# A hybrid decoder's two layers on one core: raw tiles transposed in pairs between the layers, and a memory norm shared by both

## The chip, the cores and the metric

The kernel runs on one core of one Trainium2 chip. A time is the time on the device of one execution, in microseconds (us); a profile is one more execution, recorded instruction by instruction. In the profile PE is the matrix engine (TensorE), PEld its loading of weights, DVE the vector engine (VectorE), ACT the scalar engine (ScalarE), POOL is GpSimd, and SP is SyncE, which mostly issues transfers (DMAs). Each engine works through its own instructions in order and waits on semaphores for the others.

## The reference, cut to what matters

The activations x are 512 rows of 1024 numbers in float32, the memory is 256 rows of 1024.

```python
def rmsnorm(x, g):
    y = x * rsqrt(mean(x * x, axis=-1) + EPS)
    return y * g

for layer in range(2):
    h = rmsnorm(x, g_mix_pre[layer])
    f = fox_shortconv_mixer(h, ...) if layer == 0 else rglru_mixer(h, c_w_in, ...)
    x = x + rmsnorm(f, g_mix_post[layer])
    m = rmsnorm(mem, g_mem[layer])
    f = memory_cross_attention(rmsnorm(x, g_cross_pre[layer]), m, w_xq, w_xkv, w_xo)
    x = x + rmsnorm(f, g_cross_post[layer])
    f = swiglu(rmsnorm(x, g_ffn_pre[layer]), w_ffn_gu, w_ffn_down)
    x = x + rmsnorm(f, g_ffn_post[layer])
```

Layer 0 mixes with forgetting attention and a short convolution, layer 1 with a recurrent block whose first step is the product of h with `c_w_in` (1024 x 2048). The memory `mem` is the same in both layers; only the weights `g_mem[layer]` differ.

## The kernel before

**Numbers.** Every product of matrices is made in three: each operand is split into a high part (a copy in the matrix format, made by ACT: `hTh`, `wh`, `rh`, `mTh`) and a low part (operand minus high part, made by DVE: `hTl`, `wl`, `rl`, `mTl`), and PE runs high x high, high x low and low x high into one bank of PSUM (`mm3`).

**Tiles.** x stays in SBUF as four tiles of 128 rows, `x[0]` to `x[3]`. A norm takes the sum of squares of each half of a row (`junk` on ACT), two small DVE operations and a power on POOL (`rstd`; its name is `pre` or `post`), and then a scaling on DVE, `scaled` (L256), which multiplies by the row's factor and by the norm's weights in one operation per 512 columns. The scaled rows `h` are transposed by PE (`put_T`, L303, two banks of 4 transposes for a tile), and ACT and DVE split each bank of 128x512 at once (L312, L313). `half 0` below is tiles 0 and 1, `half 1` is tiles 2 and 3; a group of 24 matmuls of 128x256 makes one bank of a half.

**The output stage.** `DownProj.run` is the last product of a layer. It runs the rows in pairs of tiles, over a sequence of groups for which a table `at[g]` says what ACT and DVE do beside PE's matmuls of group g. The last groups (`late`) are run tile by tile at its end: tile 2's remainder, then tile 3's. c is the sum of a part of the result, `gain` multiplies it by the weights of the norm behind it (`yb` is such a product), `root` is `rstd`, `add` adds it to x (L813). In layer 0 (`more`) the stage goes on into the first product of layer 1: it squares, scales and transposes each new tile of x, and loads and splits the first weights of `c_w_in` in four pieces n = 0 to 3 (`hi_f` is load and cast on ACT, L777, `lo_f` the difference on DVE, L781). `hook(m)` is called by that product after its group m of half 0 and transposes tiles 2 and 3; group m = 3 is the last, then half 1 begins. In layer 1 (`final`) `add` also writes the output.

**The memory.** In each layer `memory_rows` loads and normalizes the memory, and `memory_T` transposes it (two steps of 8 transposes of 128x128, L971) and splits it; the steps run within the mixer's output product.

**Order.** In these stages each engine runs its instructions in the order in which the code issues them; the tables and the order of calls set it. Buffers come from rings: an instruction that writes to a buffer waits until the last reader of its earlier content is done. Loads of weights are issued by SP, each as soon as its buffer is free.

Of the kernel before, what the change touches and what calls it, by code (L numbers as in the profile page):

```python
# [15 lines left out]
P = 128  # L16
# [4 lines left out]
MEM = 256  # L21
# [21 lines left out]
def trunk_kernel(ctx: ExitStack, tc: tile.TileContext, a: dict, out: bass.AP):  # L43
# [103 lines left out]
    def spend(n, behind=None):  # L147
# [14 lines left out]
        ("scw", a["ab_conv_w"][0].rearrange("j (m p) -> (j m) p", p=P)),  # L162
    )
# [135 lines left out]
    def put_T(hT, t, hs, bank=bankB):  # L299
        for hf in range(2):  # L300
            ps = bank()
            for j in range(4):
                nc.tensor.transpose(  # L303
                    out=ps[:, j * P:(j + 1) * P], in_=hs[hf][:, j * P:(j + 1) * P], identity=ident
                )
            v = ps.rearrange("p (k c) -> p k c", k=4)
            sl = slice(t * P, (t + 1) * P)
            if hT.raw:
                nc.scalar.copy(out=hT.raw[hf][:, :, sl], in_=v)
            hi, lo = dst_T(hT, hf, t)  # L310
            last = (
                nc.scalar.copy(out=hi, in_=v).ins,  # L312
                nc.vector.tensor_tensor(out=lo, in0=v, in1=f(hi), op=ALU.subtract).ins,  # L313
            )
        return last

# [324 lines left out]
    class DownProj(OutProj):  # L641
# [183 lines left out]

        def run(self):
# [39 lines left out]
            for t in range(2):  # L866
# [5 lines left out]
                if not self.final:  # L872
                    do(g + 2, lambda t=t: self.square_x(t))
                    do(g + 4, lambda t=t: self.root(t))
                    do(g + 5, lambda t=t: self.scale(t))
# [22 lines left out]
            if more:  # L898
                self.hi_f(0)
                self.transpose(0)  # L900
                self.hi_f(1)
# [3 lines left out]
            if more:  # L905
                self.transpose(1)
            self.gain(1, q[0], yb[0])
            self.root(2)
            if more:
                self.lo_f(0)  # L910
            self.add(2, (p1[0], yb[0]))
            if more:
                self.square_x(2)
                self.hi_f(2)
                self.lo_f(1)
                self.root(2)
                self.hi_f(3)
            for s in late[2:]:
                self.mms(s, (1,), bk[6])
            total(1)  # L920
            self.gain(1, q[1], yb[1])
            if more:
                self.scale(2)
            self.root(3)
            if more:
                self.lo_f(2)
            self.add(3, (p1[1], yb[1]))
            if more:
                self.square_x(3)
                self.lo_f(3)  # L930
                self.root(3)

        def hook(self, m):
            if m == 1:
                self.transpose(2)
                self.scale(3)
            elif m == 2:
                self.transpose(3)


    def memory_rows(layer, gate):

        with tc.issue_after(gate) if gate else nullcontext():
            g = load_gain(a["g_mem"][layer])
        mg = group("mem")
        for t in range(2):
# [8 lines left out]
            for hf in range(2):  # L955
                nc.vector.scalar_tensor_tensor(
                    out=mt[hf], in0=mt[hf], scalar=r, in1=g[hf], op0=ALU.mult, op1=ALU.mult
                )
        return mg

    def memory_T(mg, bank):

        ghi, glo = group("mTh"), group("mTl")
        vhi = ghi.rearrange("p a (b c) -> p (a b) c", c=MEM)
        vlo = glo.rearrange("p a (b c) -> p (a b) c", c=MEM)

        def step(t):
            for hf in range(2):
# [5 lines left out]
                v = ps.rearrange("p (k c) -> p k c", k=4)  # L974
                dst = (slice(None), slice(hf * 4, hf * 4 + 4), slice(t * P, (t + 1) * P))
                nc.scalar.copy(out=vhi[dst], in_=v)
                nc.vector.tensor_tensor(out=vlo[dst], in0=v, in1=f(vhi[dst]), op=ALU.subtract)

        return vhi, vlo, (lambda: step(0), lambda: step(1))
# [556 lines left out]
    for layer in range(2):  # L1536
# [11 lines left out]
        vhi, vlo, steps = memory_T(memory_rows(layer, pm.gate), pm.first)  # L1548
# [40 lines left out]
```

## Time and profile before

| | |
|---|---|
| median of 3 runs | 1395.26 us (1394.58 to 1395.35) |
| the profiled execution's own time | 1394.71 us |
| its span in the profile | 1392.9 us |
| mean granted clock of PE | 0.997 of full speed |
| PE busy | 1378.2 us, 99% of the span |
| DVE busy | 1116.3 us, 80% |
| ACT busy | 720.2 us, 52% |
| POOL busy | 111.1 us, 8% |

In a row of the timeline stand the start in us, the duration, the engine, the line of the kernel, the operation, output and inputs by name, and their size; xN is N instructions in a row, and a bracket holds the idle time of the engine just before and what ended it. In a group's row stand busy time and mean duration in ns behind the bar. The boundary between the layers lies at 710 to 750 us, the memory steps of layer 0 at 210 to 235 us, those of layer 1 at 850 to 885 us, and the last output stage ends the span. The first product of layer 1, half 0, begins at 728.5 us.

### The profile page before, as it was taken

Reading aid. Unit: us, or ns where it says so; the run is one execution under the profiler, and the core shown is the slowest. Engines: PE = TensorE matmul, PEld = TensorE weight load, DVE = VectorE, ACT = ScalarE, POOL = GpSimd, SP = SyncE. Lnnn points to the kernel's source line nnn. Section 1 sums busy time; section 2 is a strip of 40 time slices with the busy share of each in tenths; the row PEclk is TensorE's granted clock in tenths of the full one; section 3 lists DMA queues with packets and bytes.
Section 4 is the critical chain, followed back from the end, with each engine's and each line's share of the span. In section 5 each row is a group of like instructions: output and inputs, shape, how many; then the busy total and the mean of one; then the engine's idle time right before and its main releaser. Section 6 shows DMA issues by size and latency. Waiting matters only on the chain.

```text
span 1392.9 us, 21792 instructions
## 1 busy us (share of the span) xinstructions
PE 1378.2 (99%) x8432; PEld 1227.8 (88%) x8432; DVE 1116.3 (80%) x1801; ACT 720.2 (52%) x1175; POOL 111.1 (8%) x162
## 2 busy tenths in 40 slices
PE   8999999999999999999999999999999999999998
PEld 6778788888899999998879888888889999999886
DVE  6876678546589999989898998754558999999987
ACT  4354455534464444456664796543446444445663
POOL 1000001012010101000010000101200010000001
PEclk9999999999999999999999999999999999999999
DMA  6845452669224557567656657267822555656664
GB/s 224 277 155 159 137 181 57 202 164 177 66 92 142 163 143 196 160 241 222 195 159 210 222 181 242 73 199 163 164 67 91 166 150 151 177 168 233 205 188 144
DMA packets 156066, 233.61 MB, mean 168 GB/s; under 512 B 8549, under 2 KB 90545, under 8 KB 154938
## 3 DMA queue, kind: packets, MB, share of 16 engines
q1 hardware_dynamic: 135138, 180.25, 40.3%
q0 software_dynamic: 16928, 45.11, 15.0%
q10 hardware_dynamic: 3896, 6.86, 1.5%
q8 instruction: 66, 1.08, 0.3%
q14 instruction: 38, 0.31, 0.1%
HBM read 220.64 MB, written 57.69 MB: 200 GB/s over the span
## 4 chain that ended last, share of the span: by engine, by line
PE 95%; DVE 3%; issue 1%; DMA 1%; ACT 0%; POOL 0%; SPq 0%; DVEq 0%; POOLq 0%; ACTq 0%
PE bA L319 14%; PE bA L321 14%; PE bA L320 14%; PE bB L319 6%; PE bB L320 6%; PE bB L321 6%; PE bB L795 2%; PE bB L794 2%; PE bB L793 2%; PE bA L552 2%; PE bA L554 2%; PE bB L554 2%; PE bA L553 2%; PE bB L553 2%; PE bB L552 2%; PE bA L795 2%
## 5 line engine op out<-in xcount | busy, mean ns | idle before, releaser
L529 DVE TENSOR_TENSOR wl<-st,wh 128x1024 fp32r<-128x1024 f32 x108 | 131.4, 1222 | 99.1 <-ACT wh L528 98.1
L528 ACT CAST wh<-st 128x1024 fp32r<-128x1024 f32 x108 | 113.4, 1051 | 122.4 <-PE bA L320 70.6
L319 PE MATMUL bA<-hTh,wh 128*128 128x512 f32 (+1 forms) x448 | 171.9, 384 | 0.0
L321 PE MATMUL bA<-hTh,wl 128*128 128x512 f32 (+1 forms) x448 | 168.9, 377 | 2.3 <-DVE wl L781 2.3
L320 PE MATMUL bA<-hTl,wh 128*128 128x512 f32 (+1 forms) x448 | 168.2, 375 | 0.0
L420 ACT CAST wg<-wr 128x1024 fp32r<-128x1024 f32 x80 | 83.7, 1046 | 49.2 <-DVE wr L449 38.5
L759 ACT CAST wh<-st 128x1024 fp32r<-128x1024 f32 x76 | 74.9, 985 | 63.6 <-PE bA L795 27.0
L321 PEld LDWEIGHTS bA<-hTh,wl 128*128 128x128 f32 x448 | 84.8, 189 | 18.4 <-DVE wl L781 2.8
L421 DVE TENSOR_TENSOR wg<-wr,wg 128x1024 fp32r<-128x1024 f32 x80 | 97.4, 1217 | 0.0
L320 PEld LDWEIGHTS bA<-hTl,wh 128*128 128x128 f32 x448 | 85.0, 190 | 13.6
L319 PEld LDWEIGHTS bA<-hTh,wh 128*128 128x128 f32 x448 | 85.0, 190 | 13.4
L764 DVE TENSOR_TENSOR wl<-st,wh 128x1024 fp32r<-128x1024 f32 x76 | 86.7, 1140 | 10.1 <-ACT wh L759 10.1
L420 ACT CAST wh<-tt 128x1024 fp32r<-128x1024 f32 x40 | 42.1, 1053 | 61.5 <-DVE tt L449 61.5
L319 PE MATMUL bA<-hTq,wh 128*128 128x256 f32 x208 | 59.2, 284 | 0.0
L321 PE MATMUL bA<-hTq,wl 128*128 128x256 f32 x208 | 58.8, 283 | 0.0
L320 PE MATMUL bA<-hTq,wh 128*128 128x256 f32 x208 | 58.8, 283 | 0.0
L793 PE MATMUL bB<-wh,ya 128*128 128x512 f32 x148 | 57.6, 389 | 0.0
L794 PE MATMUL bB<-wl,ya 128*128 128x512 f32 x148 | 57.6, 389 | 0.0
L795 PE MATMUL bB<-wh,ya 128*128 128x512 f32 x148 | 57.6, 389 | 0.0
L739 DVE TENSOR_TENSOR ya<-yb,ya 128x512 fp32r<-128x512 f32 x84 | 53.9, 645 | 0.0
L793 PE MATMUL bA<-wh,ya 128*128 128x512 f32 x132 | 51.3, 389 | 0.0
L794 PE MATMUL bA<-wl,ya 128*128 128x512 f32 x132 | 51.3, 389 | 0.0
(372 smaller groups left out, 4434.8 us busy)
## 6 DMA issues: line engine op xcount, KB each, us to landing
wr<-in_w_ffn_gu_dram SPq DMA_DIRECT2D x80, 512.0 KB, 5.5
st<-t SPq DMA_DIRECT2D x40, 512.0 KB, 4.2
t<-in_w_ffn_down_dram SPq DMA_DIRECT2D x32, 512.0 KB, 5.1
st<-in_w_xkv_dram SPq DMA_DIRECT2D x32, 512.0 KB, 4.7
st<-in_w_ffn_down_dram SPq DMA_DIRECT2D x30, 512.0 KB, 3.4
st<-in_ab_w_in_dram SPq DMA_DIRECT2D x24, 512.0 KB, 4.7
y<-yr POOLq DMA_DIRECT2D x18, 512.0 KB, 4.2
t<-in_w_ffn_down_dram POOLq DMA_DIRECT2D x16, 512.0 KB, 8.4
```

Source lines behind the costliest of these rows:

```text
L319: nc.tensor.matmul(out=ps, lhsT=wh, rhs=xh, start=first, stop=False)
L320: nc.tensor.matmul(out=ps, lhsT=wh, rhs=xl, start=False, stop=False)
L321: nc.tensor.matmul(out=ps, lhsT=wl, rhs=xh, start=False, stop=last)
L420: return (lambda: nc.scalar.copy(out=to[0], in_=src), lambda: nc.vector.tensor_tensor(out=to[1], in0=src, in1=f(to[0]), op=ALU.subtract))
L421: lambda: nc.vector.tensor_tensor(out=to[1], in0=src, in1=f(to[0]), op=ALU.subtract))
L528: nc.scalar.copy(out=hi, in_=src)
L529: nc.vector.tensor_tensor(out=lo, in0=src, in1=f(hi), op=ALU.subtract)
L759: nc.scalar.copy(out=self.wt[s][0], in_=self.st[s])
L764: nc.vector.tensor_tensor(out=lo, in0=self.st[s], in1=f(hi), op=ALU.subtract)
L793: nc.tensor.matmul(out=banks[t], lhsT=yh, rhs=wh[:, jj, :], start=first and jj == 0, stop=False)
L794: nc.tensor.matmul(out=banks[t], lhsT=yh, rhs=wl[:, jj, :], start=False, stop=False)
L795: nc.tensor.matmul(out=banks[t], lhsT=yl, rhs=wh[:, jj, :], start=False, stop=last and jj == n - 1)
```

## The change

- **Pairs of raw tiles (layer 0's output stage).** Tiles 0 and 1 are scaled by ACT with the row's factor alone (`scale_raw`). `put_T_pair` transposes two blocks of 128 columns of both tiles into one bank, four times (j = 0 to 3), and ACT and DVE split each block k in a 128x256 operation of its own, which also multiplies by the weight of the norm ("gp", one number per partition).
- **The next weights.** `hi_f` 0 and 1 move ahead of the squares of the last sums; `lo_f` 0 and 1 come ahead of the first pairs, pieces 2 and 3 later.
- **The order of the tail.** The last matmuls (`late[2:]`) are issued ahead of the gain of tile 2, `total(1)` ahead of `add(2)`, in both layers; in layer 0 `scale(2)` comes behind `add(3)`, and the hook runs one group later.
- **The memory.** Layer 0 scales the rows by the row's factor alone, keeps the transposed rows as `mTr`, writes them to DRAM (`memT`, 1 MB) and splits `mTr` with the weights of `g_mem[0]` ("gm") in 8 parts. Layer 1 loads `memT` and splits it with those of `g_mem[1]`; its norm and its transposes are gone, as are the loads of g_mem spread over all partitions.

```diff
@@ vectors loaded at the start, one number per partition
+        ("gm", a["g_mem"].rearrange("l (m p) -> (l m) p", p=P)),
+        ("gp", a["g_mix_pre"][1].rearrange("(m p) -> m p", p=P)),
...
+    def put_T_pair(hT, hss, j, gain):
+        ps = bankB()
+        for kk in range(2):
+            for t in range(2):
+                c = 2 * kk + t
+                src = hss[t][j // 2][:, (j % 2 * 2 + kk) * P:(j % 2 * 2 + kk + 1) * P]
+                nc.tensor.transpose(out=ps[:, c * P:(c + 1) * P], in_=src, identity=ident)
+        for kk in range(2):
+            k, v = 2 * j + kk, ps[:, kk * 256:kk * 256 + 256]
+            hi, lo, g = hT.hi[k][:, 0:256], hT.lo[k][:, 0:256], ch(gain, k)
+            nc.scalar.mul(out=hi, in_=v, mul=g)
+            nc.vector.scalar_tensor_tensor(out=lo, in0=v, scalar=g, in1=f(hi), op0=ALU.mult, op1=ALU.subtract)
...
+        def scale_raw(self, t):
+            self.hs[t] = [sbuf("h") for _ in range(2)]
+            for hf, h in enumerate(self.hs[t]):
+                nc.scalar.mul(out=h, in_=x[t][:, hf * 512:(hf + 1) * 512], mul=self.r[t])
...
-                    do(g + 5, lambda t=t: self.scale(t))
+                    do(g + 5, lambda t=t: self.scale_raw(t))
+            if not self.final:
+                do(6 * N + 1, lambda: [self.hi_f(n) for n in range(2)])
...
             if more:
-                self.hi_f(0)
-                self.transpose(0)
-                self.hi_f(1)
+                for n in range(2):
+                    self.lo_f(n)
+                self.pairs(0, 1)
             for s in late[:2]:
                 self.mms(s, (1,), bk[6])
             total(0)
             if more:
-                self.transpose(1)
+                for n in range(2):
+                    self.hi_f(2 + n)
+                self.lo_f(2)
+                self.pairs(2, 3)
+            for s in late[2:]:
+                self.mms(s, (1,), bk[6])
             self.gain(1, q[0], yb[0])
             self.root(2)
+            total(1)
             if more:
-                self.lo_f(0)
+                self.lo_f(3)
             self.add(2, (p1[0], yb[0]))
             if more:
                 self.square_x(2)
-                self.hi_f(2)
-                self.lo_f(1)
-                self.root(2)
-                self.hi_f(3)
-            for s in late[2:]:
-                self.mms(s, (1,), bk[6])
-            total(1)
             self.gain(1, q[1], yb[1])
-            if more:
-                self.scale(2)
             self.root(3)
             if more:
-                self.lo_f(2)
+                self.root(2)
             self.add(3, (p1[1], yb[1]))
             if more:
                 self.square_x(3)
-                self.lo_f(3)
+                self.scale(2)
                 self.root(3)
...
         def hook(self, m):
-            if m == 1:
+            if m == 2:
                 self.transpose(2)
                 self.scale(3)
-            elif m == 2:
+            elif m == 3:
                 self.transpose(3)
...
-                nc.vector.scalar_tensor_tensor(
-                    out=mt[hf], in0=mt[hf], scalar=r, in1=g[hf], op0=ALU.mult, op1=ALU.mult
-                )
+                nc.vector.tensor_scalar_mul(out=mt[hf], in0=mt[hf], scalar1=r)
...
+        raw = f(group("mTr")).rearrange("p a (b c) -> p (a b) c", c=MEM)
+        if layer:
+            nc.sync.dma_start(out=raw, in_=memT)
+        else:
+            mg = memory_rows()
+        def parts(ks):
+            for k in ks:
+                g = ch("gm", 8 * layer + k)
+                nc.scalar.mul(out=vhi[:, k, :], in_=raw[:, k, :], mul=g)
+                nc.vector.scalar_tensor_tensor(
+                    out=vlo[:, k, :], in0=raw[:, k, :], scalar=g, in1=f(vhi[:, k, :]), op0=ALU.mult, op1=ALU.subtract
+                )
+        def last():
+            turn(1)
+            nc.gpsimd.dma_start(out=memT, in_=raw)
+            parts(range(KT))
+        if layer:
+            return vhi, vlo, (lambda: parts(range(4)), lambda: parts(range(4, KT)))
+        return vhi, vlo, (lambda: turn(0), last)
```

What this moves on DVE at the boundary between the layers: before, from the sum of the last groups of half a tile (c from bA) on; tile 0 and 1's differences are `hTl<-bB,hTh` of 128x4x128, the weights' are `wl<-st,wh`.

```order
849 L828 TENSOR_TENSOR c_6439<-bA,c_6439 128x512 x2
850 L804 TENSOR_TENSOR c_6439<-c_6439,gain 128x512 x2
851 L313 TENSOR_TENSOR hTl<-bB,hTh 128x4x128 x2
852 L828 TENSOR_TENSOR c_6439<-bB,c_6439 128x512
853 L313 TENSOR_TENSOR hTl<-bB,hTh 128x4x128 x2
854 L804 TENSOR_TENSOR yb<-c_6439,gain 128x512
855 L222 TENSOR_SCALAR post<-post 128x1
856 L226 SCALAR_TENSOR_TENSOR post<-post 128x1
857 L781 TENSOR_TENSOR wl<-st,wh 128x1024
858 L813 SCALAR_TENSOR_TENSOR x_112<-c_6439,post,x_112 128x512
859 L813 SCALAR_TENSOR_TENSOR x_112<-yb,post,x_112 128x512
```

After the change, on DVE from the same sum on:

```order
845 L849 TENSOR_TENSOR c_6452<-bA,c_6452 128x512 x2
846 L820 TENSOR_TENSOR c_6452<-c_6452,gain 128x512 x2
847 L797 TENSOR_TENSOR wl<-st,wh 128x1024 x2
848 L331 SCALAR_TENSOR_TENSOR hTl<-bB,chan,hTh 128x256 x4
849 L849 TENSOR_TENSOR c_6452<-bB,c_6452 128x512
850 L797 TENSOR_TENSOR wl<-st,wh 128x1024
851 L331 SCALAR_TENSOR_TENSOR hTl<-bB,chan,hTh 128x256 x4
852 L820 TENSOR_TENSOR yb<-c_6452,gain 128x512
853 L224 TENSOR_SCALAR post<-post 128x1
854 L228 SCALAR_TENSOR_TENSOR post<-post 128x1
855 L849 TENSOR_TENSOR c_6452<-bB,c_6452 128x512
856 L797 TENSOR_TENSOR wl<-st,wh 128x1024
```

Two weight differences now stand ahead of the first difference of the activations, and the sum of tile 3 (row 855) ahead of the addition to x of tile 2. ACT at the same place, before (`junk,post` are the squares of the sums):

```order
429 L218 ACTIVATE junk,post<-c_6439 128x512 x2
430 L777 CAST wh<-st 128x1024
431 L312 CAST hTh<-bB 128x4x128
432 L107 DMA gain<-in_g_mem_dram 128x512
433 L312 CAST hTh<-bB 128x4x128
434 L777 CAST wh<-st 128x1024
435 L218 ACTIVATE junk,post<-c_6439 128x512
436 L312 CAST hTh<-bB 128x4x128 x2
```

And ACT there after the change, from the raw scaling of tile 1 on:

```order
430 L845 ACTIVATE h<-x_111,pre 128x512 x2
431 L775 CAST rh<-st 128x512
432 L793 CAST wh<-st 128x1024 x2
433 L220 ACTIVATE junk,post<-c_6452 128x512 x2
434 L330 ACTIVATE hTh<-bB,chan 128x256
435 L107 DMA gain<-in_g_cross_pre_dram 128x512
436 L330 ACTIVATE hTh<-bB,chan 128x256 x3
437 L220 ACTIVATE junk,post<-c_6452 128x512
438 L793 CAST wh<-st 128x1024 x2
439 L330 ACTIVATE hTh<-bB,chan 128x256 x4
```

Two weight casts have moved ahead of the squares, and the casts of the activations come in eight parts with two weight casts and a square between the fourth and the fifth. On DVE at the end of the kernel (layer 1's output stage), before:

```order
1571 L828 TENSOR_TENSOR c_13055<-bB,c_13055 128x512
1572 L804 TENSOR_TENSOR yb<-c_13055,gain 128x512
1573 L222 TENSOR_SCALAR post<-post 128x1
1574 L226 SCALAR_TENSOR_TENSOR post<-post 128x1
1575 L813 SCALAR_TENSOR_TENSOR x_112<-c_13055,post,x_112 128x512
1576 L813 SCALAR_TENSOR_TENSOR x_112<-yb,post,x_112 128x512
1577 L828 TENSOR_TENSOR c_13055<-bB,c_13055 128x512
1578 L804 TENSOR_TENSOR yb<-c_13055,gain 128x512
```

The same place after the change:

```order
1558 L849 TENSOR_TENSOR c_13041<-bB,c_13041 128x512
1559 L820 TENSOR_TENSOR yb<-c_13041,gain 128x512
1560 L224 TENSOR_SCALAR post<-post 128x1
1561 L228 SCALAR_TENSOR_TENSOR post<-post 128x1
1562 L849 TENSOR_TENSOR c_13041<-bB,c_13041 128x512
1563 L829 SCALAR_TENSOR_TENSOR x_112<-c_13041,post,x_112 128x512
1564 L829 SCALAR_TENSOR_TENSOR x_112<-yb,post,x_112 128x512
1565 L820 TENSOR_TENSOR yb<-c_13041,gain 128x512
```

The last sum, which follows PE's last matmul, has moved from behind the two additions to x of tile 2 (`x_112`) to ahead of them.

More of the change, by code (lines that the diff above doesn't have):

```diff
@@ L929, in run, with pairs, memory_rows @@
                 self.square_x(3)
-                self.lo_f(3)
+                self.scale(2)
                 self.root(3)
+        def pairs(self, *js):
+            for j in js:
+                put_T_pair(self.hT, self.hs, j, "gp")
         def hook(self, m):
-            if m == 1:
+            if m == 2:
                 self.transpose(2)
                 self.scale(3)
-            elif m == 2:
+            elif m == 3:
                 self.transpose(3)
-    def memory_rows(layer, gate):
-        with tc.issue_after(gate) if gate else nullcontext():
-            g = load_gain(a["g_mem"][layer])
+    memT = dram.tile([P, KT, MEM], F32, name="memT")
+    def memory_rows():
         mg = group("mem")
@@ L955, in memory_rows, with memory_T @@
             for hf in range(2):
-                nc.vector.scalar_tensor_tensor(
-                    out=mt[hf], in0=mt[hf], scalar=r, in1=g[hf], op0=ALU.mult, op1=ALU.mult
-                )
-        return mg
-    def memory_T(mg, bank):
+                nc.vector.tensor_scalar_mul(out=mt[hf], in0=mt[hf], scalar1=r)
+        return mg
+    def memory_T(layer, bank):
+        raw = f(group("mTr")).rearrange("p a (b c) -> p (a b) c", c=MEM)
         ghi, glo = group("mTh"), group("mTl")
@@ L965, in memory_T, with turn @@
         vlo = glo.rearrange("p a (b c) -> p (a b) c", c=MEM)
-        def step(t):
+        if layer:
+            nc.sync.dma_start(out=raw, in_=memT)
+        else:
+            mg = memory_rows()
+        def turn(t):
             for hf in range(2):
@@ L973, in step @@
                     )
[L974 to L979, printed above, removed]
+                nc.scalar.copy(out=raw[:, hf * 4:hf * 4 + 4, t * P:(t + 1) * P], in_=ps.rearrange("p (k c) -> p k c", k=4))
+        def parts(ks):
[12 more added lines that the diff above has]
+        return vhi, vlo, (lambda: turn(0), last)
     def memory_kv(layer, vhi, vlo, between):
@@ L1547, in trunk_kernel @@
             rglru(hT, prev, pm)
-        vhi, vlo, steps = memory_T(memory_rows(layer, pm.gate), pm.first)
+        vhi, vlo, steps = memory_T(layer, pm.first)
         pm.half1(steps)
```

## The prediction

> **What bounds the kernel now.** I read the page's first part, then the chain that ended last, the waits of the TensorE (PE), and then the timelines of the three places that the change touches.
>
> ```profile
> PE 1378.2 (99%) x8432; PEld 1227.8 (88%) x8432; DVE 1116.3 (80%) x1801; ACT 720.2 (52%) x1175; POOL 111.1 (8%) x162
> ...
> PE 95%; DVE 3%; issue 1%; DMA 1%; ACT 0%; POOL 0%; SPq 0%; DVEq 0%; POOLq 0%; ACTq 0%
> ```
>
> PE is busy 99% of the span and 95% of the chain. So only three things can move the end: fewer PE instructions, fewer waits of PE, and a shorter tail after its last matmul. What PE waits for, in total:
>
> ```profile
> PE bB L303 <- DVE h L256: 2.5, 4, 1.1
> PE bA L321 <- DVE wl L781: 2.3, 2, 1.8
> ```
>
> The second row is the boundary between the layers, the stage that the change rewrites, and of the first row 0.84 us lies there. PE at the boundary, and the clock that it was granted in it:
>
> ```profile
> 725.55 1.03 PE L303 MATMUL bB<-ident,h 128*128 128x128 f32 x8
> ...
> 730.70 0.38 PE L321 MATMUL bA<-hTh,wl 128*128 128x256 f32 x1 [1.80 <-DVE wl L781]
> ...
> 733.69 0.58 PE L321 MATMUL bA<-hTh,wl 128*128 128x256 f32 x1 [0.50 <-DVE wl L781]
> 738.29 1.04 PE L303 MATMUL bB<-ident,h 128*128 128x128 f32 x8
> 743.23 1.23 PE L303 MATMUL bB<-ident,h 128*128 128x128 f32 x8 [0.84 <-DVE h L256]
> 744.21 0.36 PE L319 MATMUL bA<-hTh,wh 128*128 128x256 f32 x1
> ...
> 747.04 0.28 PE L321 MATMUL bA<-hTh,wl 128*128 128x256 f32 x1
> ```
> ```profile
> 730.00:732.00 2.00, 1.30 (x8) 1.30 (x9) 1.56 (x3) 0.07 (x1) 1.05 (x1) 0.81 0.06 15
> 732.00:734.00 2.00, 1.50 (x7) 1.20 (x7) 1.89 (x5) 1.97 (x5) 0.00 (x0) 0.50 0.92 298
> ...
> 744.00:746.00 2.00, 2.00 (x19) 2.00 (x18) 1.29 (x2) 1.07 (x2) 0.12 (x2) 1.00 0.96 320
> ```
>
> The rows at 744.21 and 747.04 are the first and last of 24 matmuls, 0.12 us apart; half 1 (tiles 2 and 3) begins behind the last, at 747.2. In the windows the seventh number is the granted clock: 0.50 after the stall of 1.80 us. DVE is what PE waits for; its rows there, and those of ACT and the loads:
>
> ```profile
> 713.19 1.41 DVE L256 SCALAR_TENSOR_TENSOR h<-x,pre,gain 128x512 f32<-128x512 f32 x2
> ...
> 720.45 1.28 DVE L828 TENSOR_TENSOR c<-bA,c 128x512 f32<-128x512 f32 x2
> 721.98 1.45 DVE L804 TENSOR_TENSOR c<-c,gain 128x512 f32<-128x512 f32 x2 [0.25 <-ACT junk L218]
> 724.16 1.29 DVE L313 TENSOR_TENSOR hTl<-bB,hTh 128x512 fp32r<-128x512 f32 x2 [0.73 <-ACT hTh L312]
> ...
> 729.43 1.22 DVE L781 TENSOR_TENSOR wl<-st,wh 128x1024 fp32r<-128x1024 f32 x1
> ...
> 735.21 1.41 DVE L256 SCALAR_TENSOR_TENSOR h<-x,pre,gain 128x512 f32<-128x512 f32 x2
> ...
> 742.33 1.41 DVE L256 SCALAR_TENSOR_TENSOR h<-x,pre,gain 128x512 f32<-128x512 f32 x2
> ```
> ```profile
> 721.23 0.63 ACT L218 ACTIVATE junk<-c 128x512 bf16<-128x512 f32 x1 [5.26 <-DVE c L828]
> ...
> 722.61 1.03 ACT L777 CAST wh<-st 128x1024 fp32r<-128x1024 f32 x1
> ```
> ```profile
> 716.02 15.08 SPq L119 DMA_DIRECT2D st<-in_c_w_in_dram  x5
> ```
> ```profile
> st<-in_w_ffn_down_dram SPq DMA_DIRECT2D x30, 512.0 KB, 3.4
> ...
> st<-in_c_w_in_dram SPq DMA_DIRECT2D x16, 512.0 KB, 5.4
> ```
>
> **The boundary, step by step.** Prices: a 128x512 scalar_tensor_tensor on DVE takes 0.75 us, a 128x256 operation from PSUM 0.42, and ACT's 128x256 with a pointer operand 0.47, by these groups:
>
> ```profile
> L813 DVE SCALAR_TENSOR_TENSOR x<-c,post,x 128x512 f32<-128x512 f32 x12 | 8.6, 748 | 1.8 <-POOL post L230 1.8
> L468 DVE TENSOR_TENSOR wy<-bA,wx 128x256 f32<-128x256 f32 x40 | 16.9, 422 | 6.4 <-PE bA L321 6.2
> L1047 ACT ACTIVATE p<-bB,sm 128x256 f32<-128x256 f32 x32 | 14.8, 474 | 17.1 <-DVE sm L1044 17.1
> ```
>
> No row shows the new DVE split (one pointer, one PSUM and one SBUF tensor, 128x256). I take 0.45; between half of 0.75 and 0.5, the eight cost within 0.6 us of that.
>
> DVE loses the four scalings of tiles 0 and 1 (two pairs of 1.41) ahead of 720.45, and ACT, idle for 5.26 us there, gains them (raw, without the weights of the norm). But the two c additions still wait for PE's last matmul of their banks, so DVE idles instead. What it does bring: the buffers of the c_w_in loads come free earlier: the first at 714.9 instead of 716.02, the second at 716.4. A load lands after 3.4 to 5.4 us by the two rows; I take 4.6. So the second weight cast, now ahead of the squares on ACT, runs 721.0 to 722.1. The two squares (0.75 with the read of the accumulator) follow, DVE's two gains wait for them and end at 724.2, and the two weight differences (1.14 each in sequence) at 726.5. Before, tile 0's differences stood there.
>
> Only then come the split parts of pairs 0 and 1. In each bank ACT's k+1 waits for DVE's k and DVE's k+1 for ACT's k+1, about 0.55 for each hand-over of 0.45 to 0.5: k=0 to 3 take 726.5 to 729.4. PE reaches pair 2 at 725.55, but its bank is freed by k=1 at 728.0: PE waits 2.5 us, and a further 1.0 for pair 3. No transposition is cheaper: eight before, eight now, in both places.
>
> ACT then takes a square (730.1 to 730.9, behind DVE's c), two weight casts (to 732.8), and k=4 to 7 go back and forth until 736.2. PE has finished the residual matmuls by 732 and the first k=0 to 3, and ends the first group of 24 matmuls at 736.6; before, it ended 24 matmuls ahead of 738.29, at 735.4. DVE goes on with yb, root, c, a weight difference, x2, yb, two roots: 741.8. x3 now stands ahead of the scaling of tile 2: x3 742.0 to 743.3, h2 until 744.7, its transposes at 744.2, where PE, two groups of 24 further, would be at 742.4 (a wait of 1.8). hTl until 746.7, h3 until 748.0, tile 3's transposes at 748.2. Since no 24 matmuls follow them now, the cast (0.6) and the difference (0.7) of tile 3 lie open: half 1 begins at 750.1 instead of 747.2.
>
> The same steps over the old order give 746.75, so that I take the difference of two reckonings: +3.4 us. Bounds: with loads at 3.4 and hand-overs of 0.45, about 1.2 and 0.8 less, +1.4; with loads at 5.4 and 0.65 each, +5.
>
> **Memory, layer 1.** Its 16 transposes are gone:
>
> ```profile
> L971 PE MATMUL bB<-ident,mem x16: 272/273/273, 873.0 to 880.1; 128*128 128x128 f32 x16
> ```
>
> Eight in a row are 1.04 us in the rows above, with the last one's 0.27 overlapping the next: (1.04 - 0.27) / 7 = 0.11 each, so 16 x 0.11 = -1.76 us of PE, all on the path. The statistics, squares and scalings go from engines that PE does not wait for, worth 0. Eight ACT and eight DVE parts (3.3 us each) come instead, on ACT around the casts of the next weights; ACT is 52% busy, and the load of 1 MB replaces four with the same bytes on SP. 0, with a bound of +1 if ACT waits for that load.
>
> **Memory, layer 0.** The tile memT is written by one transfer on POOL's queue, issued at about 222, and the second half of tile 0's hTl takes the buffer that it reads. DVE waits there for the write, and everything behind it.
>
> ```profile
> 225.43 1.28 DVE L313 TENSOR_TENSOR hTl<-bA,hTh 128x512 fp32r<-128x512 f32 x2
> ...
> 227.77 1.42 DVE L256 SCALAR_TENSOR_TENSOR h<-x,pre,gain 128x512 f32<-128x512 f32 x2 [0.73 <-POOL pre L230]
> ```
> ```profile
> 229.91 1.03 PE L303 MATMUL bA<-ident,h 128*128 128x128 f32 x8
> ```
> ```profile
> t<-in_w_ffn_down_dram POOLq DMA_DIRECT2D x16, 512.0 KB, 8.4
> ...
> yb<-y POOLq DMA_DIRECT2D x8, 1024.0 KB, 5.4
> ```
>
> With 5.4 us the write lands at 227.4, and DVE, 1.2 us later than before by the finer parts, is there at 226.8. From hTl's start to the first half of h are 0.69 + 0.35 + 0.73 + 0.75 = 2.5, so 229.9, when PE wants it: 0. With 8.4 it would be 3. I take +0.1, since the 1 MB row is the same size and queue.
>
> **The end.** Run also by the last stage: PE's last sum, c, now stands ahead of x2.
>
> ```profile
> 1384.47 0.75 DVE L813 SCALAR_TENSOR_TENSOR x<-yb,post,x 128x512 f32<-128x512 f32 x1
> 1386.13 0.69 DVE L828 TENSOR_TENSOR c<-bB,c 128x512 f32<-128x512 f32 x1 [0.91 <-PE bB L795]
> 1386.86 0.69 DVE L804 TENSOR_TENSOR yb<-c,gain 128x512 f32<-128x512 f32 x1
> ...
> 1389.21 0.75 DVE L813 SCALAR_TENSOR_TENSOR x<-yb,post,x 128x512 f32<-128x512 f32 x1
> ```
>
> x2 was done while DVE waited for PE; now its two operations (0.67 apart) come between c and yb: +1.3, of which 0.1 is regained at the root, whose squares no longer come last: +1.2. Bounds 1.0 and 1.4. The two small loads more at the start (gm, gp) run on ACT's queue beside the loads of x; I put them at 0.
>
> **Sum.** 3.4 - 1.76 + 0.1 + 1.2 = +2.9. The profiled execution took 1394.71 (a span of 1392.9 and 1.8 around it), so 1397.7; it lies 0.55 below the median of 1395.26, and I add the sum to the median: 1398.2. A change of under 0.2% (2.8 us) can hardly be told from none here, so the forecast lies on that border.
>
> **A page against the rows.** The Trainium skill, "TensorE: Matmul & The Clock Gate", section "Why this matters for your kernels", says to avoid PE gaps over about 3 us, since one idle window halves the clock. By that, gaps of 2.5 and 1.8 would cost only themselves. The trace does not agree: 1.80 us sufficed for 0.50 in the windows, while after 0.84 the clock stayed 1.00. By the page the sum stays +2.9; by the row at 732 it could become +5.1 (the third rival).
>
> **Rivals.**
> - Faster: the early split does what it could, and PE's stalls of 1.80, 0.50 and 0.84 go, with half of the slow clock's cost: -3.1 at the boundary, -3.7 in all, 1391.6 or, with 0.6 left, about 1392. It needs the first four parts done by 725.5, thus weight differences done at 722.6, 3.9 us before my reckoning. Against it speaks ACT's order: squares behind a cast that waits for a load. Chance 0.15.
> - The same: alternation and loads at their short ends, +1.4: +0.9, 1396.2. Chance 0.26.
> - The clock: after a wait of 1.8 for h2, the next 24 matmuls at 0.21 instead of 0.12 are 2.2 us more, right ahead of tile 3: 1400.4. For it speaks the 0.50 row; against it, that a clock slowed already by the pair's wait of 2.5 leaves PE later and the wait for h2 near 0.8. Chance 0.12.
> - The write of memT is late (8.4): 1401.1. Chance 0.05.
> - My forecast, within 1.2 of 1398.2: 0.42.
>
> Over 1398.05 lie half of the forecast's share and a little more (0.28), the clock and the write: 0.45. Faster 0.15, same 0.40. The range is 1394.6 to 1401: below it are the faster case, above it a late write with a slow clock.
>
> **What would show it.** Right: a PE wait of over 1.5 us for DVE at the pair's transposes of 725.6, another at tile 2's, half 1 at 750; no memory transposes near 873; c, x2, x2, yb at the end. Wrong: pair 2 without a wait, half 1 before 747, or a DVE wait for a DMA near 227.

## The result, and the profile after

The changed kernel takes **1398.12 us** (median of 16 runs, 1397.24 to 1399.05), the kernel before beside it 1395.31 (16 runs, 1394.58 to 1396.87): a ratio of 1.0019, with a 95% interval of 1.0012 to 1.0027. It is 2.8 us slower (1.7 to 3.8 by the interval). 1398.2 was predicted. The total is right, in part by luck: below it, the boundary's term was 0.8 us too high in the profiled execution, and 0.8 us that had been put at nothing came at the start of the span and at its end.

The profiled execution took 1397.59 us, with a span of 1395.8. The page's first part, and its chain that ended last by engine:

```profile
PE 1377.8 (99%) x8416; PEld 1227.0 (88%) x8416; DVE 1111.7 (80%) x1801; ACT 725.8 (52%) x1187; POOL 109.9 (8%) x161
...
PE 94%; DVE 3%; DMA 1%; issue 1%; ACT 1%; POOL 0%; SPq 0%; DVEq 0%; POOLq 0%; ACTq 0%
```

PE has 16 instructions fewer and is busy 0.4 us less, yet the span is 2.9 us longer: the time went into waits and into the tail. PE's waits by total:

```profile
PE bB L326 <- DVE hTl L331: 3.3, 2, 2.5
PE bB L305 <- DVE h L258: 2.6, 3, 1.2
...
PE bA L336 <- DVE hTl L315: 0.3, 1, 0.3
PE bA L335 <- ACT hTh L314: 0.2, 1, 0.2
```

The old boundary row (2.3 us for the weight difference wl) is gone; the transposes of the pairs (L326) wait 3.3 us in its place, and half 1 waits for its split (L335, L336), which it did not before. The same places in PE's timeline:

```profile
722.47 1.04 PE L326 MATMUL bB<-ident,h 128*128 128x128 f32 x8
...
728.76 0.63 PE L326 MATMUL bB<-ident,h 128*128 128x128 f32 x4 [2.50 <-DVE hTl L331]
730.18 0.63 PE L326 MATMUL bB<-ident,h 128*128 128x128 f32 x4 [0.79 <-DVE hTl L331]
...
744.31 1.38 PE L305 MATMUL bB<-ident,h 128*128 128x128 f32 x8 [1.23 <-DVE h L258]
...
748.41 1.03 PE L305 MATMUL bB<-ident,h 128*128 128x128 f32 x8
749.68 0.38 PE L335 MATMUL bA<-hTh,wh 128*128 128x256 f32 x1 [0.24 <-ACT hTh L314]
750.41 0.39 PE L336 MATMUL bA<-hTl,wh 128*128 128x256 f32 x1 [0.34 <-DVE hTl L315]
```

Why the pairs are late stands in ACT's and DVE's rows of the same time:

```profile
721.77 1.05 ACT L793 CAST wh<-st 128x1024 fp32r<-128x1024 f32 x1 [1.63 <-DMA st<-in_c_w_in_dram]
722.73 0.62 ACT L220 ACTIVATE junk<-c 128x512 bf16<-128x512 f32 x1
...
724.11 0.46 ACT L330 ACTIVATE hTh<-bB,chan 128x256 fp32r<-128x256 f32 x1
...
727.62 0.84 ACT L330 ACTIVATE hTh<-bB,chan 128x256 fp32r<-128x256 f32 x2 [3.06 <-DVE hTl L331]
729.04 0.47 ACT L330 ACTIVATE hTh<-bB,chan 128x256 fp32r<-128x256 f32 x1 [0.58 <-DVE hTl L331]
```
```profile
723.48 1.45 DVE L820 TENSOR_TENSOR c<-c,gain 128x512 f32<-128x512 f32 x2 [3.41 <-ACT junk L220]
724.84 2.35 DVE L797 TENSOR_TENSOR wl<-st,wh 128x1024 fp32r<-128x1024 f32 x2
727.11 0.48 DVE L331 SCALAR_TENSOR_TENSOR hTl<-bB,chan,hTh 128x256 fp32r<-128x256 f32 x1
728.13 0.88 DVE L331 SCALAR_TENSOR_TENSOR hTl<-bB,chan,hTh 128x256 fp32r<-128x256 f32 x2 [0.54 <-ACT hTh L330]
729.55 0.48 DVE L331 SCALAR_TENSOR_TENSOR hTl<-bB,chan,hTh 128x256 fp32r<-128x256 f32 x1 [0.54 <-ACT hTh L330]
```

ACT waits 1.63 us for a load of `c_w_in` before its second cast; the squares stand behind that cast, DVE's c behind the squares (3.41 idle), and two weight differences (2.35) behind c. Only at 727.11 does the first low part begin, and then ACT and DVE take turns, each waiting 0.54 to 0.58 for the other. PE's granted clock (the seventh number) in the same stretch:

```profile
730.00:732.00 2.00, 1.82 (x8) 1.56 (x9) 0.63 (x2) 1.27 (x3) 0.00 (x0) 0.70 1.06 375
732.00:734.00 2.00, 2.00 (x6) 1.52 (x6) 1.49 (x2) 1.70 (x3) 0.00 (x0) 0.50 0.71 272
734.00:736.00 2.00, 2.00 (x17) 1.96 (x16) 1.10 (x3) 1.17 (x3) 0.00 (x0) 0.94 0.60 176
...
744.00:746.00 2.00, 1.59 (x12) 1.39 (x13) 1.52 (x5) 1.36 (x4) 0.60 (x4) 1.00 0.31 110
```

Behind the waits of 2.50 and 0.79 the clock falls to 0.50, as it did before behind 1.80; after that of 1.23 at tile 2 it stays at 1.00. What the first three windows lack, 0.30 + 0.50 + 0.06 of 2 us each, is a stretch of 3.4 us at half clock; before (0.81, 0.50 and 0.83) it was as long.

Layer 0's memory: DVE's rows around the write of memT, and that write among the page's DMA issues (the last number is the median from issue to landing).

```profile
226.88 0.69 DVE L315 TENSOR_TENSOR hTl<-bA,hTh 128x512 fp32r<-128x512 f32 x1
227.73 0.69 DVE L315 TENSOR_TENSOR hTl<-bA,hTh 128x512 fp32r<-128x512 f32 x1 [0.16 <-DMA memT<-mTr]
...
229.50 1.41 DVE L258 SCALAR_TENSOR_TENSOR h<-x,pre,gain 128x512 f32<-128x512 f32 x2 [0.75 <-POOL pre L232]
```
```profile
memT<-mTr POOLq DMA_DIRECT2D x1, 1024.0 KB, 4.8
```

DVE does wait for the write, but for 0.16 us, and PE shows no wait there: its transposes of tiles 0 and 1 come 0.64 and 0.65 us later than before (224.19 and 230.56, against 223.55 and 229.91), close to the 0.60 that it has been later since 30 us.

DVE's rows at the end:

```profile
1387.50 0.69 DVE L849 TENSOR_TENSOR c<-bB,c 128x512 f32<-128x512 f32 x1 [3.00 <-PE bB L811]
1388.10 0.74 DVE L829 SCALAR_TENSOR_TENSOR x<-c,post,x 128x512 f32<-128x512 f32 x1
1388.76 0.74 DVE L829 SCALAR_TENSOR_TENSOR x<-yb,post,x 128x512 f32<-128x512 f32 x1
1389.43 0.69 DVE L820 TENSOR_TENSOR yb<-c,gain 128x512 f32<-128x512 f32 x1
...
1391.78 0.75 DVE L829 SCALAR_TENSOR_TENSOR x<-yb,post,x 128x512 f32<-128x512 f32 x1
```

DVE idles 3.00 us before the last c with tile 2's two operations still to do, and does them behind it.

**Segments.** All kernels of this study can be compared between four points that each of them has: the boundary's first transposes (722 us), the second matmul of half 1 (the first that needs hTl), layer 1's transposes behind the memory steps (883 us), and the last operation on x. Times in us, from one profiled execution each:

| kernel | boundary | to layer 1's transposes | to the last x |
|---|---|---|---|
| before | 25.34 | 135.69 | 506.24 |
| after | 27.94 | 133.93 | 507.44 |
| after_again | 27.24 | 133.93 | 507.43 |
| tail_back | 26.88 | 133.92 | 506.23 |
| boundary_alone | 27.48 | 135.72 | 506.25 |
| memory_alone | 27.02 | 133.83 | 506.45 |
| squares_first | 24.95 | 133.92 | 507.42 |
| hi_then_lo | 25.88 | 133.92 | 507.40 |
| both | 22.71 | 133.91 | 507.41 |
| hook_back | 31.23 | 133.83 | 507.41 |
| before_warm | 25.36 | 135.63 | 507.58 |
| before_warm_once | 25.34 | 135.69 | 506.22 |
| best | 22.84 | 133.92 | 506.23 |
| best_no_memory | 22.80 | 135.72 | 506.26 |

So the profiled execution of after has +2.60, -1.76 and +1.20 = +2.04 of its own. The other 0.53 of the last x's shift (1389.21 to 1391.78) was there when the boundary began, and the span ends 0.3 later behind the last x than before (3.3 instead of 3.0). The store of the last result is not longer: its last packet ends 1.7 behind that x in both. Behind it SyncE goes through ten final waits, about 0.06 apart. In before the wait for this store comes last, in after five more follow it.

### The profile page after: what moved, and what is told of

Read it like the earlier page. It is cut to its first block, busy times and chain, and to the rows that moved or that the text cites. A ratio compares the mean times of both kernels' runs of the same rounds, so it can differ in the third digit from the quotient of the medians.

```text
span 1395.8 us, 21761 instructions
## 1 busy us (share of the span) xinstructions
PE 1377.8 (99%) x8416; PEld 1227.0 (88%) x8416; DVE 1111.7 (80%) x1801; ACT 725.8 (52%) x1187; POOL 109.9 (8%) x161
## 4 chain that ended last, share of the span: by engine, by line
PE 94%; DVE 3%; DMA 1%; issue 1%; ACT 1%; POOL 0%; SPq 0%; DVEq 0%; POOLq 0%; ACTq 0%
PE bA L335 14%; PE bA L337 14%; PE bA L336 14%; PE bB L336 6%; PE bB L335 6%; PE bB L337 6%; PE bB L811 2%; PE bB L809 2%; PE bB L810 2%; PE bA L568 2%; PE bA L570 2%; PE bB L570 2%; PE bA L569 2%; PE bB L569 2%; PE bB L568 2%; PE bA L811 2%
## 5 line engine op out<-in xcount | busy, mean ns | idle before, releaser
L335 PE MATMUL bA<-hTh,wh 128*128 128x512 f32 (+1 forms) x448 | 171.4, 383 | 0.2 <-ACT hTh L314 0.2
L336 PE MATMUL bA<-hTl,wh 128*128 128x512 f32 (+1 forms) x448 | 167.8, 375 | 0.3 <-DVE hTl L315 0.3
L336 PEld LDWEIGHTS bA<-hTl,wh 128*128 128x128 f32 x448 | 84.6, 189 | 14.2 <-DVE hTl L315 0.5
L335 PEld LDWEIGHTS bA<-hTh,wh 128*128 128x128 f32 x448 | 84.6, 189 | 14.0 <-ACT hTh L314 0.5
L335 PE MATMUL bA<-hTq,wh 128*128 128x256 f32 x208 | 59.2, 284 | 0.0
L336 PE MATMUL bA<-hTq,wh 128*128 128x256 f32 x208 | 58.8, 283 | 0.0
```

Of the source, the lines that this page charges most:

```text
L335: nc.tensor.matmul(out=ps, lhsT=wh, rhs=xh, start=first, stop=False)
L336: nc.tensor.matmul(out=ps, lhsT=wh, rhs=xl, start=False, stop=False)
```

## The experiments

Each kernel was timed beside the kernel before on the same chip. That had medians of 1395.74 (33 runs), 1396.31 (28), 1395.64 (22) and 1395.76 (15) in the four groups, with intervals of the ratio of about 0.0009 to each side (1.2 us). The groups ran on different chips, so kernels of different groups are compared below by what each differs from the before beside it. The second and the third segment repeat to about 0.2 us where nothing is changed and decide below the certainty of the medians. The boundary does not repeat so: with the same code it took 26.88 to 27.94.

### Group 1: the parts one by one

**after_again** is the changed kernel itself.

> The changed kernel itself, beside which the others of this call stand. Against the kernel before: +2.0 to +2.9 us by both theories. Theory A (the boundary between the layers costs +2.6, the memory steps -1.76, the end +1.2): +2.0. The profile so far had +0.6 more at the start, ahead of all that the change touches; by theory A that is chance and comes out on either side here, by the rival (the two small loads more at the start cost it) it is there again.

1398.23 us (11 runs; ratio 1.0013, 1.0004 to 1.0022), +2.49. In its profile the pairs wait 1.82 and 0.79, and tile 2 waits 1.33. The later start is there again: the transposes of layer 0 near 30 us come at 30.59, against 30.06 in before. This run alone can't tell the small loads from chance; the start is taken up again below.

**tail_back**: in the last stage alone, the sum of the last part is again behind tile 2's addition.

```diff
-            total(1)
+            if more:
+                total(1)
             if more:
                 self.lo_f(3)
...
+            else:
+                total(1)
```

> The changed kernel, with the sum of tile 3 behind the addition to x of tile 2 again in the last output stage alone. Theory A: -1.2 us against the changed kernel, all behind the last matmul. Rival: the end of the kernel is set by the output transfers and not by DVE; then the four transfers only lie differently and it is within 0.3.

1396.67 us (11 runs; ratio 1.0001, 0.9992 to 1.0010): 1.56 less than after_again. Its DVE rows at the end show the mechanism:

```profile
1384.27 0.75 DVE L829 SCALAR_TENSOR_TENSOR x<-c,post,x 128x512 f32<-128x512 f32 x1 [0.68 <-POOL post L232]
1384.94 0.75 DVE L829 SCALAR_TENSOR_TENSOR x<-yb,post,x 128x512 f32<-128x512 f32 x1
1386.60 0.69 DVE L849 TENSOR_TENSOR c<-bB,c 128x512 f32<-128x512 f32 x1 [0.91 <-PE bB L811]
...
1389.68 0.74 DVE L829 SCALAR_TENSOR_TENSOR x<-yb,post,x 128x512 f32<-128x512 f32 x1
```

Tile 2's pair is done before PE ends, and the last segment is 506.23 instead of 507.43: 1.20, as predicted. Of the 1.56 in medians the other 0.36 lies within the uncertainty.

**boundary_alone**: the kernel before with the new boundary only, without the shared memory norm and with the old tail.

> The kernel before with the new boundary between the layers alone (pairs, early weights, order, hooks; memory and last stage as before). Theory A: +2.6 us against the kernel before. Rival: the boundary is neutral and the loss is at the start and the end: within 0.5.

1397.78 us (11 runs; ratio 1.0012, 1.0003 to 1.0020), +2.04. The rewritten boundary alone makes the kernel slower; its segment is 27.48, +2.14.

**memory_alone**: the kernel before with only the shared memory norm.

> The kernel before with the shared memory norm alone. Theory A: -1.8 us against the kernel before (16 transposes fewer on TensorE, 0.11 each), and TensorE's transposes of tile 0 in layer 1 come 1.8 earlier than before, counted from the transposes of tile 0 at the boundary. Rival: the parts that ScalarE and VectorE have to make instead, and the wait for the transfer, take it back: 0. By the rival for the start, the gm load alone shows as +0.3 at 30 us.

1395.52 us (11 runs; ratio 0.9994, 0.9985 to 1.0002): -0.2, where -1.8 was expected. The interval, -2.1 to +0.3, holds both. The segment in which the transposes are gone did shrink, by 1.86. In its profiled execution the time was lost again at the boundary, whose code is that of before: 27.02 against 25.34. The windows there:

```profile
732.00:734.00 2.00, 1.55 (x12) 1.26 (x11) 1.90 (x3) 1.03 (x3) 0.07 (x1) 0.78 0.61 190
734.00:736.00 2.00, 1.30 (x6) 1.30 (x7) 1.85 (x5) 2.00 (x4) 0.55 (x1) 0.50 0.80 261
736.00:738.00 2.00, 2.00 (x11) 2.00 (x11) 1.89 (x6) 0.92 (x3) 0.00 (x0) 0.50 1.09 313
738.00:740.00 2.00, 2.00 (x12) 2.00 (x11) 1.56 (x2) 0.00 (x0) 1.46 (x1) 0.52 0.95 301
```

Behind a wait of 1.78 us, with a second one of 1.15 following, PE was granted half its clock for 6.8 us (0.22 + 0.50 + 0.50 + 0.48 of 2 us each), against 3.4 in the profile of before behind 1.80 and 0.50. PE came so late to tile 2's transposes that ACT idled 4.88 before it could split them (3.01 in before) and DVE idled 0.94 and 0.34 behind ACT's squares, so the lost clock reached the end. This profile explains one execution (1396.11 us); that the median lost the same way is not shown by it. best_no_memory, below, asks again.

### Group 2: the order at the boundary

Three reasons for the slower boundary were to be told apart: DVE's chain (squares behind a cast that waits for a load, and the alternation of ACT and DVE), the later places of tiles 2 and 3 (`hook`), and the clock.

**squares_first**: the second weight cast goes behind the squares of c.

```diff
-                do(6 * N + 1, lambda: [self.hi_f(n) for n in range(2)])
+                do(6 * N + 1, lambda: self.hi_f(0))
...
+            if not self.final:
+                do(6 * N + 1, lambda: self.hi_f(1))
```

> The changed kernel, with the second weight cast on ScalarE behind the two squares of the sums instead of ahead of them. Theory A: VectorE's gains no longer wait for a square behind a cast that waits for its load; weight differences are done 1.5 to 2.3 us earlier, the wait at the pair's transposes falls from 2.5 to under 1, and half 1 begins 1.5 to 2.3 earlier: -1.5 to -2.3 us against the changed kernel. Rival B (the order behind the pairs, x3 ahead of the scaling of tile 2, and the hooks one group later set the loss): the wait moves to tile 2's transposes, within 0.4 of the changed kernel.

1395.68 us (11 runs; ratio 0.9995, 0.9986 to 1.0004): -0.63 from the before beside it, where after_again had +2.49, so about 3.1 less, more than the 1.5 to 2.3 that were expected. The boundary is 24.95, 1.9 to 3.0 less than with the order of after. DVE's gains now wait 0.42 for the squares instead of 3.41; PE's wait at the first late pair is gone, and that at the next is 0.49:

```profile
720.66 1.45 DVE L820 TENSOR_TENSOR c<-c,gain 128x512 f32<-128x512 f32 x2 [0.42 <-ACT junk L220]
```
```profile
727.37 0.63 PE L326 MATMUL bB<-ident,h 128*128 128x128 f32 x4 [0.49 <-DVE hTl L331]
```

**hi_then_lo**: in each bank ACT makes both high parts, then DVE both low parts.

```diff
+        los = []
         for kk in range(2):
...
             nc.scalar.mul(out=hi, in_=v, mul=g)
+            los.append((lo, v, g, hi))
+        for lo, v, g, hi in los:
             nc.vector.scalar_tensor_tensor(out=lo, in0=v, scalar=g, in1=f(hi), op0=ALU.mult, op1=ALU.subtract)
```

> The changed kernel, with both high parts of a pair's bank issued ahead of both low parts, so that ScalarE and VectorE don't hand each k to each other. Theory A: each pair of pairs takes 1.8 us on VectorE instead of 2.9: -2.2 us against the changed kernel. Rival B: within 0.4.

1395.64 us (11 runs; ratio 0.9995, 0.9986 to 1.0004): -0.67 from the before beside it, so about 3.2 less than after_again, where 2.2 were expected. Its DVE rows show what the turns had cost:

```profile
725.82 2.35 DVE L800 TENSOR_TENSOR wl<-st,wh 128x1024 fp32r<-128x1024 f32 x2
728.09 1.65 DVE L334 SCALAR_TENSOR_TENSOR hTl<-bB,chan,hTh 128x256 fp32r<-128x256 f32 x4
```

Four low parts take 1.65 in one piece; in after they took from 727.11 to 730.03, 2.92. PE still waits 2.01 for the first late pair, because the weight differences end as late as in after, and the clock is halved for 3.4 us behind it. The boundary is 25.88.

**both** edits together.

> The changed kernel with both edits (second weight cast behind the squares, high parts of a bank ahead of its low parts). Theory A: -3.7 to -4.5 us against the changed kernel if the two add, and TensorE's wait at the pair's transposes is under 0.8. Rival B: within 0.5.

1393.20 us (11 runs; ratio 0.9977, 0.9968 to 0.9986): -3.11 from the before beside it, so about 5.6 less than after_again, more than the 3.7 to 4.5 expected. The two add: on top of squares_first the order of the parts takes the boundary from 24.95 to 22.71. No transpose of a pair waits, and PE's clock is 1.00 in all windows from 724 to 740. What PE waits for is tile 2:

```profile
PE bB L305 <- DVE h L258: 2.7, 3, 1.3
```

**hook_back**: tiles 2 and 3 are transposed one group of matmuls earlier again, as before the change.

```diff
-            if m == 2:
+            if m == 1:
...
-            elif m == 3:
+            elif m == 2:
```

> The changed kernel with the transposes of tiles 2 and 3 one group earlier again, as before. Theory A: VectorE's scaling of tile 2 sets the time, TensorE waits for it 2.9 us longer at the earlier place, and only the cast of tile 3 is covered: +1.7 to +1.9 us against the changed kernel. Rival B (the later hooks cost the uncovered cast): -0.9.

1400.72 us (6 runs; ratio 1.0031, 1.0020 to 1.0043): +4.41 from the before beside it, so about 1.9 more than after_again. The later hooks are not what costs; they cover a part of DVE's lateness. PE's timeline, and two windows behind the wait:

```profile
744.16 1.97 PE L305 MATMUL bB<-ident,h 128*128 128x128 f32 x8 [4.22 <-DVE h L258]
750.31 1.04 PE L305 MATMUL bB<-ident,h 128*128 128x128 f32 x8
```
```profile
744.00:746.00 2.00, 1.84 (x9) 1.83 (x10) 1.06 (x5) 0.94 (x3) 0.72 (x6) 0.50 0.33 108
746.00:748.00 2.00, 2.00 (x11) 2.00 (x11) 1.84 (x3) 0.59 (x1) 0.10 (x1) 0.50 0.00 0
```

From tile 2's transposes to tile 3's are 6.15 us, against 4.10 in after (744.31 to 748.41) for the same matmuls. Tile 3's transposes wait for nothing here, so the halved clock lies on the path and its price can be read: 2.05 us.

### Group 3: the clock, and the best version

**before_warm**: the kernel before with 14 idle transposes of the identity in front of the matmul that waits for the weight difference at the boundary. The function is used in three places, and so the transposes were added three times, two of them (at 396 and 1057 us) where PE had no wait to fill.

> The kernel before with 14 idle transposes of the identity (0.11 each) put where TensorE waits 1.8 us for the first weight difference between the layers; they write what the next matmul overwrites. Theory C (the wait itself is covered, since VectorE sets tile 3's time; what it costs is the half clock that follows, of one or two windows): the granted clock stays 1.00 from 728 to 742, and the executions over 1396.6 us, which the kernel before has by the dozen, are gone: median 0.3 to 1.5 us lower. Rival (the two groups of times have another cause, as at the start): as many over 1396.6 as before, and the median within 0.3 or later by up to 1.5, the work added.

1398.85 us (11 runs; ratio 1.0020, 1.0011 to 1.0028). The two other places cost PE 14 x 0.11 = 1.54 each by this reckoning, and 1395.77 is left; by the third segment, which holds one of them and grew by 1.34, it is 1396.2. Either way there is no gain. A kernel with the transposes in the one place settles it:

**before_warm_once**: the idle transposes at the boundary alone.

```diff
-    def ws_gemm_split(wss, hT, hook):
+    def ws_gemm_split(wss, hT, hook, warm=0):
...
+        for _ in range(warm):
+            nc.tensor.transpose(out=banks[0][0][:, 0:P], in_=ident, identity=ident)
```

> As the kernel with the idle transposes, but with them at the boundary between the layers alone; that kernel had them in two more places, where TensorE had no wait and each cost their 1.54 us. Theory C: clock 1.00 from 728 to 742, no execution over 1396.6 us, the median 0.3 to 1 us under the kernel before. Rival (the slower executions have another cause): executions over 1396.6 us in the kernel before's proportion, the median within 0.3.

1395.66 us (11 runs; ratio 0.9998, 0.9989 to 1.0007): no change of the median, where some tenths to 1 us were expected. The clock was kept, and PE's wait filled, but tile 3 waits for DVE exactly as long as before:

```profile
730.10 1.69 PE L378 MATMUL bA<-ident 128*128 128x128 f32 x14
732.29 0.39 PE L321 MATMUL bA<-hTh,wl 128*128 128x256 f32 x1 [0.27 <-DVE wl L783]
735.28 0.39 PE L321 MATMUL bA<-hTh,wl 128*128 128x256 f32 x1 [1.29 <-DVE pre L222]
...
744.82 1.23 PE L303 MATMUL bB<-ident,h 128*128 128x128 f32 x8 [0.84 <-DVE h L256]
```
```profile
732.00:734.00 2.00, 1.73 (x13) 1.50 (x12) 1.56 (x3) 0.48 (x1) 0.64 (x1) 1.00 0.26 73
734.00:736.00 2.00, 0.72 (x6) 0.72 (x7) 1.89 (x5) 1.97 (x6) 0.36 (x1) 1.00 0.86 272
```

The boundary takes 25.34 us at full clock as with a window at 0.50: in the profile of before the lost clock is covered by DVE's chain. Whether it costs something in other executions, the spread was to tell. Over 1396.6 us are 26 of before's 98 runs in the four groups, but 21 of these fell in groups 1 and 2; beside these two kernels it is 5 of 37, against none of their own 22 (less 2.7 to 3.08 for the first). That fits a lost clock that is sometimes longer than its cover, as in memory_alone's profile, but so few can be chance, and none of the slower runs of before was profiled: this is not shown.

**best**: both edits of group 2 and the old tail.

> The changed kernel with the second weight cast behind the squares, the high parts of a bank ahead of its low parts, and the old order in the last stage. By theory A the three add up: -1.2 us against the same without the old order at the end, which was 1393.2: 1392.0, some 3.5 to 4 us under the kernel before. Rival (what one wins is lost at the next wait): no less than 1393.

**1391.52 us** (6 runs; ratio 0.9970, 0.9958 to 0.9982): faster than before by 4.1 us and, with after_again's +2.49, than after by 6.6.

**best_no_memory**: best with the memory steps of before.

> The same with the memory steps of the kernel before. By theory A, with no half clock at the boundary to blur it, the shared memory norm is worth its 16 transposes: +1.8 us against the kernel beside it. Rival (the wait for the transfer, or something else of the memory edit, takes a part back, as the -0.2 of the memory edit alone suggests): +0.2 to +1.2.

1393.48 us (11 runs; ratio 0.9985, 0.9976 to 0.9994). Sharing the memory norm is worth 1.96 in medians here and 1.80 in the segment (135.72 to 133.92), where nothing at the boundary takes it back.

## Why the prediction was right, point by point

- **The pairs: right, by its own steps.** DVE's first low part was put at 726.5 and began at 727.11, on a PE that was 0.53 later; four alternating parts were to take 2.9 and took 2.92. Predicted waits 2.5 and 1.0, measured 2.50 and 0.79. The operation that no row showed, put at 0.45, took 0.48 alone and 0.41 in a row of four. Both causes named, ACT's squares behind the cast and the hand-overs, are shown by squares_first and hi_then_lo.
- **Tile 2 and half 1: right in kind.** The wait for h2 was to be 1.8 and was 1.23. Half 1 was to begin, its split done, at 750.1; the first matmul that needs the low part came at 750.41. That is the second of the half, so a start without gaps would lie 0.12 earlier, and without the 0.53 of the later PE at 749.8.
- **The boundary's sum: mis-sized, +3.4 for +2.60.** The failed step is "The same steps over the old order give 746.75, so that I take the difference of two reckonings". The reckoning of the new order was 0.3 too long, that of the old 0.45 too short (half 1 began at 747.2), and the difference of the two took up both errors. Against the measured 747.2 the reckoning would have given +2.9. The 0.3 arose on DVE behind the eighth low part: from there to the end of the two roots 5.6 us were put (736.2 to 741.8), and 5.2 passed (736.66 to 741.86). The steps over the old order are not written out, so where the 0.45 arose stays open. The +2.60 itself is one execution; with the same code the boundary took +1.54 to +2.60.
- **The start: put at 0, was +0.5 in this execution.** The two small loads were one candidate, but their absence does not help: the transposes of layer 0 near 30 us come at 30.06 in before and 30.66 in after, at 30.61 and 31.24 in before_warm and before_warm_once, which lack both loads, and at 30.38 to 30.88 in the others. The profiled execution of before is the earliest of all. This is variation between executions.
- **The end of the span: put at 0, was +0.3.** This is no chance. Behind the last x the span of before and of the two before_warm kernels ends 3.0 later, that of the eleven others 3.3 to 3.4. It goes by the place of the last store's wait among SyncE's ten: tenth in those three, fifth in after, third in boundary_alone (3.4), at about 0.06 a place. Only those three lack both small loads; that the loads shifted the place was not tested by itself. This 0.3 and the 0.5 at the start made up for the boundary's 0.8: that the total fits to 0.1 is luck.
- **The memory: right.** -1.76 predicted; -1.76 in after, -1.86 in memory_alone, -1.80 between best_no_memory and best. The write of memT landed in 4.8, and layer 0 paid nothing (0.1 predicted). The reservation that the step lacked is that the gain needs a boundary which does not lose it.
- **The end: right.** +1.2 predicted, +1.20 in every kernel with the new order of the tail.
- **The rivals.** The faster one did not come, but its condition was the right one: with the low parts early enough (both, best) the boundary falls to 22.7 or 22.8 and the kernel beats before. The gain that the early split could have brought, 25.34 - 22.80 = 2.5 us, was in after outweighed by the order of ACT's and DVE's work around it. The late write of memT did not occur. The clock rival did not occur at tile 2 in after (1.00 after 1.23), but did in hook_back, at 2.05 us, where 2.2 had been worked out. The rival of no change was near: its +1.4 for the boundary stands beside the +1.54 of tail_back's execution, where the load landed earliest; its short hand-overs did not come (0.54 to 0.58 of idle time at each). In the faster rival's sum the -3.1 is the three waits alone (1.80 + 0.50 + 0.84); half of the slow clock's cost, which it names, is not in it.
- **The page against the rows.** The Trainium skill, "TensorE: Matmul & The Clock Gate", "Why this matters for your kernels", advises against PE gaps over about 3 us; by that, one of 2.50 would cost only itself. The trace does not agree: the clock fell to 0.50 behind 2.50 and 0.79, as the row of before had suggested. The sum held even so, since DVE's chain covered it: PE still waited 1.23 for h2 behind the slow stretch.

The effects of the parts in medians (+2.04 for the boundary, +1.56 for the tail, -0.2 to -1.96 for the memory) add up to +1.6 to +3.4, and so to +2.8 no more closely than about 1 us. Part of that is the boundary itself, whose time hangs on a load. Four profiled executions have the same code there; in them ACT's second weight cast, which waits for the load, starts at 720.91, 721.24, 721.28 and 721.77 (tail_back, after_again, boundary_alone, after), which is 1.74, 1.38, 1.14 and 0.70 ahead of the first transposes, and the boundary takes 26.88, 27.24, 27.48 and 27.94. Each later start lengthens it by its full amount (0.36, 0.24 and 0.44, for 0.36, 0.24 and 0.46). In hi_then_lo it started 0.55 ahead, for which the order of after would have taken 28.09 by this rule, so that its 25.88 are a gain of 2.2, by this estimate. Why the load lands at other times was not settled.

## What to carry to other kernels

Splitting work finer and starting it earlier helps only if the engine that does it is free then: look at what stands ahead of the new work in the program order of each engine, and above all for work behind an instruction that waits for a load. When two engines process the halves of one bank, issue all parts of the first engine before those of the second, or each part waits for a hand-over (0.54 us here, for operations of 0.4). Where a stage's tail code is shared with the last stage, look at the last stage by itself: work moved behind an engine's final wait lengthens the end by nearly its full time (1.20 us here, for two operations 0.67 apart).

## What the runs showed of the hardware

- **The clock after a gap depends on more than its length, and it is halved in whole stretches.** By the windows, every stretch of half clock at the boundary lasts 3.4 us or twice that. One of 3.4 came behind PE waits of 1.80 (then 0.50; before), 2.50 and 0.79 (after), 1.47 and 0.79 (tail_back) and 2.01 and 0.16 (hi_then_lo). One of 6.8 came behind 1.78 and 1.15 (memory_alone) and within and behind 4.22 (hook_back). After 0.84, and after 1.20 to 1.34 at tile 2 in the profiles where that wait stands alone, the clock stayed at 1.00. Fourteen idle transposes of 0.11 us each in the gap kept it at 1.00, too, with 0.27 and 1.29 left of the waits.
- **A lost clock has no price of its own.** The same 0.50 cost nothing where another engine's chain ended later anyway (before: the boundary takes 25.34 with it, and 25.34 without it in before_warm_once), about 1.7 us in memory_alone (27.02), and 2.05 where it lay on the path (hook_back).
